# An encoder step on one core: latent keys prepared during the last projections, rotations on ACT, held columns of the output projection, and the third phase's tiles placed over x's

## The chip, the cores and the metric

The kernel runs on one core of one Trainium2 chip. What is measured is the device time of one execution in microseconds (us), given as the median of several runs. A profile of one further execution goes with it. The engines are named as in the profile: PE (TensorE matmuls), PEld (its weight loads), DVE (VectorE), ACT (ScalarE), POOL (GpSimd) and SP (SyncE, which issues all the DMAs of this kernel).

## The reference, cut to what matters

One layer of a streaming encoder runs on 592 rows: 16 meta tokens, 512 prompt frames and 64 sample frames, with 128 cached rows behind the sample. Model width is 2048. Everything is fp32.

```
h = rmsnorm(x);  z = h @ w_in                  # q, k, v of 8 "diff" heads; cq (512), ckv (256), kr (64)
cq = rmsnorm(cq); qm = cq @ w_uq               # 8 latent heads: 128 plain + 64 rotary columns each
ckv = rmsnorm(ckv); krope = rope(kr)           # both are outputs too
diff heads:   p = softmax(q1 k1 + bias) - lam softmax(q2 k2 + bias);  o = rmsnorm(p v)
latent heads: km, vm = ckv @ w_ukv;  p = softmax(qn km + rope(qr) krope);  o = p vm
x = x + concat(o_diff, o_latent) @ w_out
x = x + (silu(h2 @ w_gate) * (h2 @ w_up)) @ w_down,  h2 = rmsnorm(x);  y = rmsnorm(x)
```

## The kernel before, in words

Every fp32 operand of a matmul is held as a pair: `hi` (an fp32r copy made by ACT) and `lo` (the remainder, by one DVE subtraction). A product is three passes: hi*hi, hi*lo, lo*hi. `split` (L170) makes a pair, `mm3` (L195) issues the three passes for each half of the columns, so six matmuls for one 128x128 block of weights and 576 columns.

The work around the change has three stages.

First, the projections (`projections`, L704) go through the 8 diff heads (q, k, v columns of w_in), then through the latent columns in the order 4, 5, 6, 0, 1 (ckv, ckv, kr, cq, cq), and last through cq columns 2 and 3 together, in 16 blocks of rows; each finished block calls `release(kc)` (L814), which gives that block's room in the tile of x to something else. While they run, the attention of the diff heads is woven in.

Second, the latent stage. `query_norm` (L836) sums the squares of the four cq tiles (POOL adds, then a matmul with ones) and makes the row `rsq`. `latent_keys` (L862) splits the latents and the cache and rotates the shared key; `latent_rows` (L901) turns latents and key back into rows for the outputs, closes two pools, opens `aq` in their place and sets `named`. `heads` (L1077) then goes through the 8 latent heads: `rotary_queries` (L992) for each pair, `queries_keys` (L1023) for each head, `pair_values` (L1007) for each pair, and a spawned `latent_attend` (L1043) that makes scores in 5 blocks, then the product with the values (`probabilities_times_values`, L231). `mix_out` (L938) is the first half of the output projection (the diff heads' part): 16 columns of 8 `mm3` each, and it is the fill for all gaps.

PE's order is written out by a planner (`Streams`, L45): generators yield delays or lists of things they wait for, each has a rank, the ready one of the lowest rank goes next, and the matmuls that it issues move the planned clock. `mix_out` has rank 30, `heads` 20, the attention of a head its number. PSUM banks are planned too: `ps` (2 of them), `sp` (1), `tp` (1), `po` (1). The order of ACT, DVE, POOL and SP in these stages is chosen by the compiler; that of PE is kept as planned.

Third, from L1244, the second half of the output projection: the latent heads' results are loaded from `mspill`, split, and multiplied with the lower half of w_out (`fetch`, L1261), 16 columns, and the operands for the feed-forward part are made beside it. The rest (from L1309) is the feed-forward part, three quarters of the time.

`rope` (L847) makes the rotation of a tile: four DVE operations on 32 partitions each, that read one quarter and write another (times a sign and the sine), one POOL product with the cosine, one DVE addition.

Of the kernel before, what the change touches and what calls it, by code (L numbers as in the profile page):

```python
# [30 lines left out]
H = 8  # L31
# [10 lines left out]
WR_BUFS, WH_BUFS, Z_BUFS, OT_BUFS = 2, 2, 3, 4  # L42

# [87 lines left out]
def encoder_step(  # L131
# [99 lines left out]
    def probabilities_times_values(pt_b, p5, vkeys, vpast, pool, tbank, pso, pace, done):  # L231
# [19 lines left out]
        for g, blocks in enumerate((((0, 0), (0, 1), (0, 2), (0, 3)), ((1, 0), (1, 1), (1, 2), (1, 3)),  # L251
# [3 lines left out]
            yield from st.take("tp")  # L255
# [20 lines left out]
            st.give("tp", 1.9)  # L276
# [78 lines left out]
    with ExitStack() as ph:  # L355
# [271 lines left out]
        def diff_attend(h, khs, kl, vh, vl):  # L627
# [8 lines left out]
            for b in range(5):  # L636
# [30 lines left out]
                (vh[:, 5, :], vl[:, 5, :]), ap, tbank, pso, 1.0,  # L667
# [12 lines left out]
            if h < H - 1:  # L680
                store(mspill[h], o32)
            else:
                yield [released[h]]
                mixh[h], mixl[h] = (x_room(h, w, f"mx{w}{h}")[:, 0:TQ] for w in "hl")
                split(mixh[h], mixl[h], o32)
# [3 lines left out]
        def key_latent_norm():  # L689
# [6 lines left out]
            for i in range(2):  # L696
                V.scalar_tensor_tensor(zs[4 + i], zs[4 + i], gkv[:, i:i + 1], r, op0=ALU.mult, op1=ALU.mult)

# [5 lines left out]
        def projections():  # L704
            for h in range(H):
# [39 lines left out]
            for i in (4, 5, 6, 0, 1):  # L745
# [8 lines left out]
                if i == 6:  # L754
# [5 lines left out]
                    st.spawn(2, key_latent_norm())  # L760
# [23 lines left out]
            st.spawn(2, latent_keys(), [att[H - 1]])  # L784
# [6 lines left out]

        normed = []
# [6 lines left out]
        def query_latent(i, z):  # L799
            cqh[i], cql[i] = (zl.tile([P, TQ], F32R, name=f"cq{w}{i}", tag=f"q{i // 2}{i % 2}{t}")  # L800
                              for w, t in zip("hl", "sz"))
            split_scaled(cqh[i], cql[i], z, gq[:, i:i + 1])
# [3 lines left out]
            else:  # L806
                S.activation(z, z, AF.Square)
                G.tensor_tensor(sqs[0], sqs[0], z, op=ALU.add)
# [4 lines left out]

        def release(kc):  # L814

            released[kc]["done"] = True
            if kc < H - 1:
                assert att[kc]["done"]
                mixh[kc], mixl[kc] = (x_room(kc, w, f"mx{w}{kc}")[:, 0:TQ] for w in "hl")
                load(f32(mixl[kc]), mspill[kc])  # L820
                S.activation(mixh[kc], f32(mixl[kc]), AF.Copy)
                V.tensor_tensor(mixl[kc], f32(mixl[kc]), f32(mixh[kc]), op=ALU.subtract)
            elif kc == 10:
                for w, name, src in (("h", "cos", c_cos), ("l", "sin", c_sin)):
                    at_x[name] = x_room(kc, w, name, F32)
                    load(at_x[name], src)
            elif kc == 11:
                at_x["rsq"] = x_room(kc, "h", "rsq", F32)[:, 0:TQ]
                at_x["kr"] = x_room(kc, "l", "kr", F32)
            elif kc in (12, 13):  # L830
                i = kc - 12
                oth = slice(64 - i * 64, 128 - i * 64)
                rq.append([x_room(kc, w, f"rq{i}{w}")[:, 0:TQ] for w in "hl"])
                load(f32(rq[i][1][oth, :]), qmask[oth, :])

        def query_norm():  # L836
            yield 5.0
            yield from st.take("sp")
            pq = sbig("pq")
            for i in range(2):  # L840
                PE.matmul(pq[:, i, 0:QH], ones, sqs[0][:, i * QH:(i + 1) * QH], start=True, stop=True)
            v = ztile("v")[:, 0:TQ]
            V.tensor_scalar(hv(v, TQ), ev(pq, QH), 1.0 / QL, EPS, op0=ALU.mult, op1=ALU.add)
            st.give("sp", 1.5)
            rsqrt(at_x["rsq"], v)

        def rope(dst, z):  # L847
# [14 lines left out]
        def latent_keys():  # L862

            rkh = keys_room("kh0", "rkh")
# [20 lines left out]
            kr = at_x["kr"]  # L885
# [4 lines left out]
            st.give("tp", 3.0)  # L890
            rope(kr, zs[6])
# [3 lines left out]
            yield 9.0  # L895
            st.spawn(1, latent_rows())

        named = dict(done=False)
        aq, probs = [], []

        def latent_rows():  # L901

            kr = at_x["kr"]
            for j in range(5):
                o, n = tok[j]
                yield from st.take("tp")
                pn = tbank("pn")
                for i in range(2):
                    PE.transpose(pn[0:n, i * P:(i + 1) * P], zs[4 + i][:, o:o + n], ident)
                PE.transpose(pn[0:n, 256:320], kr[0:64, o:o + n], ident[0:64, 0:64])  # L910
                nn = ztile("nn")
                V.tensor_copy(nn[0:n, 0:320], pn[0:n, 0:320])
                r = min(n, NM + SEQ - o)
                store(nckv_p[o:o + r, :], nn[0:r, 0:KVL])
# [870 lines left out]
```

## Time and profile before

| | us |
|---|---|
| median of 3 runs (2456.5 to 2459.86) | 2457.34 |
| the profiled execution's own time | 2460.72 |
| its span, first to last instruction | 2458.9 |
| PE busy | 2384.6 (97%) |
| DVE busy | 1801.3 (73%) |
| ACT busy | 1162.6 (47%) |
| POOL busy | 717.9 (29%) |

The span's mean granted TensorE clock is 0.989. The latent stage begins at about 533 us of the span (end of the projections), the third stage's first matmul starts at 830.30, and the feed-forward part begins at about 938.

How to read the rows that follow. A row of the table by stretches gives a stretch's start and end, its width, the busy time of each engine with its count of instructions, the granted clock (PEclk, 1.00 is full speed), the busy share of the DMA engines and GB/s. A row of the timeline has start, duration, engine, line, operation, out<-in, shapes and count, and in brackets how long the engine had been idle before and what released it. Line L124 is a helper's line, so tiles are told apart by their names: `ps`, `sp`, `tp`, `po`, `pv`, `pq` are PSUM tiles, `mw` the weights of the latent heads, `mxh`/`mxl` the diff heads' pairs, `t` the rotated part, `kr` the rotated key, `zq`/`zr` the rotary queries, `m` the PSUM tile of the third stage.

### The profile page before, as it was taken

What the parts mean: (1) busy time and instruction counts of PE and PEld (TensorE: products, weight loads), DVE (VectorE), ACT (ScalarE), POOL (GpSimd) and SP (SyncE); (2) the same over time, 40 slices, a digit from 0 to 9 for tenths busy, and PEclk for the clock granted to TensorE, in tenths of its full rate; (3) what the DMA queues carried; (4) which work ended last, traced back from release to release, by engine and by line L of the source; (5) the groups of instructions that cost most, each with busy time, mean ns of one, the idle gap of its engine ahead of it and who ended that gap; (6) DMA issues with size and microseconds to landing.
All of it is one profiled execution on the core that took longest, in us unless ns stands there. A gap on an engine that the chain in (4) does not pass through costs nothing.

```text
span 2458.9 us, 44446 instructions
## 1 busy us (share of the span) xinstructions
PE 2384.6 (97%) x17539; PEld 2343.2 (95%) x17539; DVE 1801.3 (73%) x2828; ACT 1162.6 (47%) x2205; POOL 717.9 (29%) x550
## 2 busy tenths in 40 slices
PE   8999999988999799999999999999999999999998
PEld 7999999988999699999999999999999999999998
DVE  5665556675666478778888888788887888888874
ACT  5554544443444355445554555555555433333445
POOL 0000000010000154644545545445454322222223
PEclk9999999999999899999999999999999999999999
DMA  8533323243231454334334443443444875744332
GB/s 244 143 91 87 83 81 98 81 121 107 87 105 63 157 175 132 110 118 156 131 130 150 137 141 133 147 160 117 141 154 157 278 233 179 236 160 164 106 116 82
DMA packets 330990, 337.49 MB, mean 137 GB/s; under 512 B 22287, under 2 KB 273942, under 8 KB 330750
## 3 DMA queue, kind: packets, MB, share of 16 engines
q1 hardware_dynamic: 330782, 334.66, 42.5%
q8 instruction: 137, 2.24, 0.4%
q14 instruction: 71, 0.58, 0.1%
HBM read 264.98 MB, written 72.97 MB: 137 GB/s over the span
## 4 chain that ended last, share of the span: by engine, by line
PE 65%; DVE 4%; DMA 2%; POOL 1%; issue 1%; ACT 1%; DVEq 0%; POOLq 0%; ACTq 0%; SPq 0%
PE m L1234 35%; PE m L1238 18%; PE m L199 5%; PE ps L107 4%; DVE wl L124 1%; PE po L107 1%; PE sp L107 1%; DVE b L124 1%; DMA raw<-in_ffn_w_down 1%; PE tp L111 1%; POOL ws L1203 1%; DMA raw<-in_ffn_w_gate 1%; DMA raw<-in_ffn_w_up 1%; PE pv L107 1%; DMA x<-mspill 0%
## 5 line engine op out<-in xcount | busy, mean ns | idle before, releaser
L1234 PE MATMUL m<-b,wh 128*128 128x288 f32 x7168 | 1048.6, 295 | 6.4 <-DVE y L124 3.2
L1234 PEld LDWEIGHTS m<-b,wh 128*128 128x128 f32 x7168 | 984.7, 189 | 8.3 <-ACT wh L124 7.2
L1238 PE MATMUL m<-b,wl 128*128 128x288 f32 x3584 | 580.8, 297 | 3.0 <-DVE wl L124 2.7
L1203 POOL TENSOR_TENSOR ws<-raw 128x512 f32<-128x512 f32 (+1 forms) x258 | 374.8, 1463 | 541.7 <-DVE wl L124 275.3
L1238 PEld LDWEIGHTS m<-b,wl 128*128 128x128 f32 x3584 | 514.4, 189 | 4.6 <-DVE wl L124 4.3
L124 ACT ACTIVATE wh<-ws 128x512 fp32r<-128x512 f32 (+1 forms) x340 | 283.4, 845 | 386.6 <-PE m L1234 242.0
L124 DVE TENSOR_TENSOR wl<-ws,wh 128x512 fp32r<-128x512 f32 (+1 forms) x340 | 391.0, 1161 | 84.4 <-ACT wh L124 82.2
L124 ACT ACTIVATE wh<-raw 128x512 fp32r<-128x512 f32 x387 | 227.4, 620 | 287.6 <-PE m L1234 250.8
L124 DVE TENSOR_TENSOR wl<-raw,wh 128x512 fp32r<-128x512 f32 x387 | 357.3, 949 | 7.6 <-ACT wh L124 7.0
L107 PE MATMUL ps<-xh,wh 128*128 128x296 f32 (+1 forms) x960 | 218.0, 309 | 2.2 <-ACT wh L124 2.2
L107 PE MATMUL ps<-xl,wh 128*128 128x296 f32 (+1 forms) x960 | 209.3, 299 | 1.5 <-DVE xl L124 1.5
L124 DVE TENSOR_TENSOR y<-y,m 128x288 f32<-128x288 f32 x312 | 140.1, 451 | 91.4 <-PE m L1238 71.3
L107 PE MATMUL ps<-xh,wl 128*128 128x296 f32 (+1 forms) x928 | 201.7, 299 | 0.1
L124 DVE TENSOR_TENSOR ws<-ws,raw 128x512 f32<-128x512 f32 (+1 forms) x129 | 110.6, 860 | 76.5 <-POOL ws L1203 74.2
L107 PEld LDWEIGHTS ps<-xh,wh 128*128 128x128 f32 x960 | 156.0, 191 | 6.2 <-ACT wh L124 2.9
L107 PEld LDWEIGHTS ps<-xl,wh 128*128 128x128 f32 x960 | 156.4, 190 | 2.2 <-DVE xl L124 2.2
L107 PEld LDWEIGHTS ps<-xh,wl 128*128 128x128 f32 x928 | 150.7, 189 | 0.8 <-DVE wl L124 0.8
L124 DVE TENSOR_TENSOR wl<-wr,wh 128x1024 fp32r<-128x1024 f32 (+1 forms) x108 | 114.7, 1062 | 37.6 <-ACT wh L124 34.1
L124 ACT ACTIVATE wh<-wr 128x1024 fp32r<-128x1024 f32 (+1 forms) x110 | 101.6, 924 | 69.7 <-PE ps L107 37.6
L1422 POOL TENSOR_TENSOR c<-c,rb 128x576 f32<-128x576 f32 x44 | 70.5, 1604 | 169.0 <-ACT c L124 169.0
L630 POOL MEMSET bias<- 64x64 f32 x8 | 1.2, 144 | 384.0 <-DMA bias<-tsk 277.4
L124 ACT ACTIVATE parts<-c 128x1 fp32r<-128x1 f32 x252 | 81.2, 322 | 41.9 <-DVE c L124 36.2
(349 smaller groups left out, 3108.3 us busy)
## 6 DMA issues: line engine op xcount, KB each, us to landing
raw<-in_ffn_w_gate SPq DMA_DIRECT2D x44, 1024.0 KB, 6.1
raw<-in_ffn_w_up SPq DMA_DIRECT2D x44, 1024.0 KB, 6.3
raw<-in_ffn_w_down SPq DMA_DIRECT2D x39, 1024.0 KB, 5.5
partspill<-parts SPq DMA_DIRECT2D x126, 288.0 KB, 2.1
b<-partspill SPq DMA_DIRECT2D x126, 288.0 KB, 6.1
wr<-in_w_in SPq DMA_DIRECT2D x60, 512.0 KB, 4.1
wr<-in_w_out SPq DMA_DIRECT2D x16, 512.0 KB, 4.3
wr<-in_w_out SPq DMA_DIRECT2D x32, 256.0 KB, 3.1
```

Source lines behind the costliest of these rows:

```text
L107: self.tc.keep_in_program_order(self.pe.matmul(out, lhsT, rhs, start=start, stop=stop))
L111: self.tc.keep_in_program_order(self.pe.transpose(out, in_, identity))
L124: ins = issue(*args, **kwargs)
L199: PE.matmul(outs[i], w, x[i], start=start and p == 0, stop=stop and p == 2)
L630: G.memset(bias[0:64, 464:528], -BIG)
L1203: engine.tensor_tensor(w[:, k:k + m, :], pick(xs), pick(ys), op=op)
L1234: PE.matmul(banks[p], wh[:, k, :], x, start=first and new and k == 0 and x is hi, stop=False, skip_group_check=not new)
L1238: PE.matmul(banks[p], wl[:, k, :], hi, start=False, stop=last and k == n - 1, skip_group_check=not new)
L1422: G.tensor_tensor(g[:, f, :], g[:, f, :], rb2, op=ALU.mult)
```

## The change: what it does, and its diff

1. The latents' norm (`key_latent_norm`) is spawned after column 5 instead of 6, and makes the ckv rows (transposes, copies and stores) itself. `latent_keys` is spawned when the last diff head's scores are planned, and needs the norm. The shared key is rotated as soon as `release(7)` gave it room, its two remainders are made on POOL instead of DVE, and its rows go out in one bank. `latent_rows` becomes `latent_room`, which only swaps the pools.
2. `rope`: four copies on ACT (scale = sign) move the quarters, one DVE product with the sine on all 128 partitions, POOL's product first, one DVE addition.
3. Query norm: the squares are issued before the split, from tiles of their own; the sum uses the `tp` bank in two halves.
4. `heads`: the rotary parts are written for each head (`rotary_parts`), an even head's projections wait for the scores of head h-2 rather than of h-1, and the values of a pair come after both heads' projections. The first rotary projection uses the `sp` bank.
5. The last head: its scores alternate between `sp` and `ps` banks, its transposes between `tp` and `sp`.
6. `mix_out` holds its last two columns (HELD = 2) until all of the heads' projections and values are planned (`prepared`).
7. Rooms over x's are dealt out anew (which tile lies over which block of x), the diff heads' results are loaded at releases 8 to 14 instead of 0 to 6.
8. Third stage: its pools move from one side of the memory to the other, all tiles are laid out beforehand, the latent heads' results are loaded straight into the tile of `lo`, and the first two blocks of w_out go through rooms of their own. Later pools (`fr`, `fw`, `fs`, `fb`, `yy`) change sides too.

```diff
-            yield from st.take("tp")
+            bank, tbank = tbanks[g % len(tbanks)]
+            yield from st.take(bank)
...
+                if h == H - 1:
+                    st.spawn(2, latent_keys(), [scored[H - 1], att[H - 2]])
...
+                    if i == 5:
+                        key_norm.append(st.spawn(2, key_latent_norm()))
...
-            st.spawn(2, latent_keys(), [att[H - 1]])
+            st.spawn(1, latent_room(), [att[H - 1]])
...
-            split_scaled(cqh[i], cql[i], z, gq[:, i:i + 1])
...
-                S.activation(z, z, AF.Square)
-                G.tensor_tensor(sqs[0], sqs[0], z, op=ALU.add)
+                sq = ztile("sq")[:, 0:TQ] if i == 3 else ap.tile([P, TQ], F32, name="sq")
+                S.activation(sq, z, AF.Square)
+                G.tensor_tensor(sqs[0], sqs[0], sq, op=ALU.add)
+            split_scaled(cqh[i], cql[i], z, gq[:, i:i + 1])
...
         def rope(dst, z):
+            G.tensor_tensor(dst, z, at_x["cos"][:, c], op=ALU.mult)
             for a in range(0, P, 32):
                 b = a ^ 32
-                V.scalar_tensor_tensor(t[b:b + 32, :], z[a:a + 32, :], sign[a:a + 32, :], at_x["sin"][a:a + 32, c],
-                                       op0=ALU.mult, op1=ALU.mult)
-            G.tensor_tensor(dst, z, at_x["cos"][:, c], op=ALU.mult)
+                S.activation(t[b:b + 32, :], z[a:a + 32, :], AF.Copy, scale=sign[a:a + 32, :])
+            V.tensor_tensor(t, t, at_x["sin"][:, c], op=ALU.mult)
             V.tensor_tensor(dst, dst, t, op=ALU.add)
...
-                sub_lo(rkl[i][both[i], 0:T], kr[both[i], :], rkh[both[i], 0:T])
+                G.tensor_tensor(rkl[i][both[i], 0:T], kr[both[i], :], f32(rkh[both[i], 0:T]), op=ALU.subtract)
...
         def mix_out():
...
             for i in range(KC):
+                if i == KC - HELD:
+                    yield [prepared]
...
-                yield from st.take("sp")
-                n, W, view, vw = scores(b, sbig(), [
+                bank = "ps" if h == H - 1 and b % 2 else "sp"
+                yield from st.take(bank)
+                n, W, view, vw = scores(b, sbig() if bank == "sp" else pjt(), [
...
+            tbanks = [("tp", tbank)] + [("sp", lambda: sbig("tp2")[:, 0, :])] * (h == H - 1)
...
         def heads():
             yield 3.0
-            for h in range(H):
-                j = h // 2
-                if h % 2 == 0:
-                    yield from rotary_queries(j)
-                if h == 0:
-                    yield [named]
-                if h >= 2:
-                    yield [asked[h - 2]]
-                qk = yield from queries_keys(h)
-                lat[h] = st.spawn(h, latent_attend(h, *qk), [asked[h - 1]] if h else [])
-                yield 0.5
-                if h % 2 == 0:
+            for j in range(H // 2):
+                zr = yield from rotary_queries(j)
+                for i in range(2):
+                    h = 2 * j + i
                     if j:
-                        yield [lat[h - 1]]
-                    yield from pair_values(j)
+                        yield [asked[h - 2]]
+                    rotary_parts(i, zr)
+                    if h == 0:
+                        yield [named]
+                    qk = yield from queries_keys(h)
+                    lat[h] = st.spawn(h, latent_attend(h, *qk), [asked[h - 1]] if h else [])
+                    yield 0.5
+                if j:
+                    yield [lat[2 * j - 1]]
+                yield from pair_values(j)
+            prepared["done"] = True
...
-    ma, close_ma = pool("ma", "right")
+    ma, close_ma = pool("ma")
...
-    mixh, mixl = [], []
+    mixed = [[mx.tile([P, TQ], F32R, name=f"m{w}{h}") for w in "hl"] for h in reversed(range(H))][::-1]
...
     for h in range(H):
-        m = ma.tile([P, TQ], F32, name="x", tag="x", bufs=3)
-        load(m, mspill[8 + h])
-        mixh.append(mx.tile([P, TQ], F32R, name=f"mh{h}"))
-        mixl.append(mx.tile([P, TQ], F32R, name=f"ml{h}"))
-        split(mixh[h], mixl[h], m)
+        load(f32(mixl[h]), mspill[8 + h])
+        S.activation(mixh[h], f32(mixl[h]), AF.Copy)
+        V.tensor_tensor(mixl[h], f32(mixl[h]), f32(mixh[h]), op=ALU.subtract)
...
+            if n < 2:
+                wr, wh, wl = (bc.tile([P, 2, QH], t, name=f"b{p}_5").rearrange("p a b -> p (a b)")[
+                    :, 0:4 * P].rearrange("p (k c) -> p k c", k=4) for p, t in zip(((1, 2, 4), (5, 6, 3))[n], (F32, F32R, F32R)))
...
-    fr, close_fr = pool("fr")
-    fw, close_fw = pool("fw")
+    fr, close_fr = pool("fr", "right")
+    fw, close_fw = pool("fw", "right")
```

More of the change, by code (lines that the diff above doesn't have):

```diff
@@ L812, in encoder_step, with mix_rooms @@
         at_x = {}
+        def mix_rooms(h):
+            mixh[h] = (x_room(h, "h", f"mxh{h}") if h < 7 else x_room(7, "l", f"mxh{h}"))[:, 0:TQ]
+            mixl[h] = x_room(8 + h, "l", f"mxl{h}")[:, 0:TQ]
         def release(kc):
             released[kc]["done"] = True
[L817 to L831, printed above, removed]
+            if kc == 0:
+                at_x["rsq"] = x_room(0, "l", "rsq", F32)[:, 0:TQ]
+            elif kc in (5, 6):
+                name, src = (("cos", c_cos), ("sin", c_sin))[kc - 5]
+                at_x[name] = x_room(kc, "l", name, F32)
+                load(at_x[name], src)
+            elif kc == 7:
+                at_x["kr"] = x_room(kc, "h", "kr", F32)
+            if kc in (9, 11):
+                i = (kc - 9) // 2
@@ L993, in rotary_queries @@
             wh, wl = weights4(w_uq4[:, :, 2 * j:2 * j + 2, 128:192], [P, 4, 2, 64])
[L994 removed]
+            z = yield from q_project(wh, wl, "zq", "ps" if j else "sp")
             yield 1.5
```

170 lines of the change are left out of this document (103 added, 67 removed).

## The prediction

> **What bounds the kernel now.** I read the page's busy times first, which make PE the busiest engine by far, then cut the span into stretches, to see where PE loses time. Lost PE time is the width less busy time times granted clock, since a matmul at half clock is busy twice as long.
>
> ```profile
> core 0: us, PE busy (x) PEld busy (x) DVE busy (x) ACT busy (x) POOL busy (x), PEclk, DMA share, GB/s
> ...
> 497.00:533.00 36.00, 34.94 (x254) 33.31 (x252) 21.66 (x37) 18.45 (x32) 3.78 (x2) 1.00 0.54 161
> 533.00:580.00 47.00, 34.71 (x198) 30.66 (x197) 35.51 (x49) 15.02 (x24) 7.21 (x13) 0.85 0.33 94
> 580.00:806.00 226.00, 221.43 (x1618) 212.25 (x1616) 135.92 (x264) 92.67 (x207) 5.11 (x3) 1.00 0.28 85
> 806.00:821.00 15.00, 11.00 (x44) 7.47 (x42) 4.76 (x11) 3.89 (x11) 0.00 (x0) 0.66 0.05 20
> 821.00:835.00 14.00, 4.70 (x21) 4.73 (x22) 5.83 (x8) 5.34 (x8) 0.00 (x0) 0.51 0.75 230
> 835.00:937.00 102.00, 101.13 (x746) 99.47 (x746) 78.23 (x114) 58.00 (x113) 46.73 (x44) 1.00 0.58 178
> 937.00:950.00 13.00, 10.45 (x65) 9.86 (x64) 11.75 (x17) 7.70 (x15) 6.33 (x6) 0.87 0.59 188
> ```
>
> Lost are 1.1 us in 497:533, 17.5 in 533:580 (47 - 34.71 x 0.85), 4.6 in 580:806, 7.7 in 806:821 (15 - 11.00 x 0.66), 11.6 in 821:835 (14 - 4.70 x 0.51), 0.9 in 835:937 and 3.9 in 937:950 (13 - 10.45 x 0.87): 47 us in all. PE's work itself doesn't change, so 47 us is the most that the change can win. Three places hold 37 of them: the start of the latent stage, the last head's end, and the step into the third stage.
>
> In the first, the waits of PE and the load on DVE say why:
>
> ```profile
> PE pn L111 <- DVE nn L124: 4.3, 3, 3.0
> PE pq L107 <- POOL sqs L808: 2.7, 1, 2.7
> PE ps L107 <- DVE xo L124: 2.1, 1, 2.1
> PE pv L107 <- DVE mw L124: 1.5, 1, 1.5
> ```
>
> ```profile
> 535.00:560.00 25.00, 17.53 (x112) 16.01 (x111) 24.56 (x32) 7.08 (x13) 6.00 (x3) 0.93 0.30 88
> ```
>
> DVE is busy 24.56 of 25 us there, and three of the four longest waits end at a DVE tile. So DVE is the bound for 25 us, while PE has 16 columns of fill to draw on that it can't use: their banks and the heads behind them wait for DVE.
>
> **Part by part: the start of the latent stage.** What DVE does in 533:580, by group:
>
> ```profile
> L124 DVE SCALAR_TENSOR_TENSOR t<-zl,sign,sin 32x592 f32<-32x592 f32 x4 | 4.3, 1083 | 0.1
> L124 DVE SCALAR_TENSOR_TENSOR t<-zq,sign,sin 32x576 f32<-32x576 f32 x4 | 4.3, 1073 | 0.1
> L124 DVE TENSOR_TENSOR wl<-wr,wh 128x1024 fp32r<-128x1024 f32 x3 | 3.7, 1221 | 0.0
> L124 DVE COPY nn<-pn 128x320 f32<-128x320 f32 x4 | 2.0, 488 | 1.9 <-PE pn L111 1.9
> ```
>
> ```profile
> L124 ACT ACTIVATE rq0h<-zr 64x576 fp32r<-64x576 f32 x4 | 2.7, 686 | 15.4 <-DVE zr L124 15.4
> ```
>
> The key's rotation (4.3 us) and the row copies (2.0) move ahead of 533, where DVE has 14 us free (36 - 21.66). The first query rotation drops from 4.3 us of DVE to one product; its four copies go to ACT at about 0.69 each (the ACT row, 64 partitions; the trace has none of 32 partitions that change place, and the other near row is DVE's own 1.08; I take ACT's, since the engine is the same), 2.7 us (4.3 at the other bound) on an engine that is busy 15 of 47. So about 10 us leave DVE's 35.5, and DVE stops being the bound. The chain that is left is the query norm:
>
> ```profile
> 537.40 3.74 POOL L808 TENSOR_TENSOR sqs<-sqs,z 128x576 f32<-128x576 f32 x2 [7.87 <-ACT z L124]
> ...
> 539.92 1.85 DVE L124 SCALAR_TENSOR_TENSOR t<-zl,sign,sin 32x592 f32<-32x592 f32 x1
> ...
> 541.20 2.29 PE L107 MATMUL pq<-sqs,ones 128*128 128x288 f32 x4 [2.69 <-POOL sqs L808]
> ...
> 551.47 0.75 DVE L124 SCALAR_TENSOR_TENSOR rsq<-v,rsq 128x576 f32<-128x576 f32 x1
> ...
> 567.42 0.85 PE L107 MATMUL ps<-cqh,mw 128*128 128x288 f32 x2
> ...
> 580.06 0.23 PE L107 MATMUL sp<-km,qnh 128*128 128x144 f32 x1
> ```
>
> Squaring before splitting lets each square skip an ACT copy and a DVE subtraction of about 0.75, so POOL's two adds (1.87 each) end near 538.3 instead of 541.1. From there: the sum 1.2 us (half of the 2.29 at half clock), four DVE steps of 0.75, two ACT steps of 0.69, some handovers: `rsq` near 545 instead of 552.2. The rotation: POOL beside ACT 2.7, two DVE steps 1.5, the parts 2: near 552 head 0's projections start, which were at 567.42 behind the rows' transposes (the 4.3 us of `pn` waits, now gone). Scores start about 16 us earlier than 580.06. In between PE needs fill, and has it:
>
> ```profile
> 591.74 0.43 PE L107 MATMUL ps<-mxh,wh 128*128 128x288 f32 x2
> 592.00 0.42 PE L107 MATMUL ps<-mxl,wh 128*128 128x288 f32 x2
> ```
>
> Two matmuls take 0.265 us, so a column (48) is 6.4 us and all 16 are 102. What stays: part of the `pq` wait (0 to 2.7, I take 1, and 1 more as its halves share one bank with a DVE read between), the weights' and the `xo` wait in part (1.5), and slow clock behind them (2): 5.5 of 17.5. Gain 12.0; bounds 3 (only the norm's 3 us) and 16.
>
> The clock: no PE wait of this stretch is over 3.0 us, yet it ran at 0.85 on average, a loss of 5 us. The Trainium skill, TensorE: Matmul & The Clock Gate, "What's actually happening", says that the clock halves after an idle window of about 3.4 us. By that rule the waits that I leave over would cost no clock, and the gain would be an estimated 14; by the trace shorter gaps do it, and I keep the 2.
>
> The two subtractions moved to POOL, with the cosine product, are some 5.6 us of POOL (three times 1.87) before 533, where POOL is busy 3.78 of 36. If they came late they would hold DVE too: the quarter at 539.92, beside POOL's adds, took 1.85 us, against a mean of 1083 ns for the four. The Trainium skill, SBUF — State Buffer, "Who interferes with whom", says that a DVE instruction with two SBUF inputs and a POOL instruction that reads SBUF share a port, and whichever starts later waits for the whole of the other; the trace agrees with that one row. By it the two subtractions would take up to an estimated 3.7 us from the gain if they met DVE's busy stretch. I take 0, because DVE has 14 us free where they run, and keep 3.7 for the range.
>
> **The projections' end.** Ten row transposes, five copies and six stores move in ahead of 533, the diff heads' loads move later. The nearest rows are the `pn` waits, at most 4.3 us if all came along; between two of them lies fill here. I take a loss of 0.8, bounds 0 and 4.3. Release 14 instead of 6 is 8 blocks of 12 matmuls later, 12.7 us. The last of these loads has one block (1.6 us) and six `mm3` of the first column (4.8) as cover; it needs a load and a split, 4.7 us by the rows of the third stage below. Without that cover it costs these 4.7.
>
> **The middle.** Two held columns take 12.8 us of fill out of 580:806. Against that an even head's projections no longer wait for the head before, so more of the heads' own work is ready at a time. I take a loss of 0.9, bounds 12.8 and a gain of 3.
>
> **The last head.** PE runs out of fill near 806 and then goes from wait to wait through the product with the values. With two held columns (12.8 us) against 7.7 lost, and banks that alternate, nearly all is covered: gain 7.0, bounds 3 and 7.7.
>
> **The step into the third stage.**
>
> ```profile
> 820.82 0.32 SPq L124 DMA_DIRECT2D mspill<-o  x1
> 823.04 1.27 SPq L124 DMA_DIRECT2D x<-mspill  x3
> ...
> 830.30 0.82 PE L199 MATMUL m<-mh,wh 128*128 128x288 f32 x2 [9.77 <-DMA x<-mspill]
> ```
>
> ```profile
> x<-mspill SPq DMA_DIRECT2D x8, 288.0 KB, 3.3
> ```
>
> Before, all the loads of the third stage stand in SP's queue behind the last head's store: 2.2 us to land, then 7.3 us until the first matmul, and the clock of 821:835 is 0.51. After, seven of the eight results and the first two weight blocks lie in rooms that are free earlier, and can be loaded and split under the last head. Only the eighth still goes out and back: store 2.2, load 3.3, split 1.4 (0.69 on ACT, 0.75 on DVE), so 6.9 us, against 42 matmuls on the other seven (5.6 us) and whatever is left of the fill. I leave 2.5 of 11.6: gain 9.1, bounds 1.5 and 11.6.
>
> **The feed-forward part.** Pools change sides; its 3.9 us at 937:950 may move by up to 2.6 either way, I take 0. No other step changes.
>
> Sum: 12.0 - 0.8 - 0.9 + 7.0 + 9.1 = 26.4 us. The profiled execution took 2460.7 (span 2458.9 and 1.8 around it), so 2434.3 for one like it; the median of the runs is 3.4 lower, so 2431.
>
> **Rivals.** (A) The fill runs out before the held columns are let go, and PE stands for those 12.8 us in the middle. For: the earlier start takes more fill before 580, and 580:806 has only 4.6 us of slack as it is. Against: with projections ready earlier the heads need less of it. 2431 + 12.8 = 2444.
>
> (B) The third stage's loads still wait for the last store, because the spill is seen as one thing or SP's queue has them in that order. For: all three loads left together 2.2 us after the store. Against: their rooms change, and one queue entry that waits would look the same. It leaves 1.5 of 9.1: 2439.
>
> (C) Slower: the values of a pair come after the odd head's projections, and the even head's product waits for them.
>
> ```profile
> 780.87 0.28 PE L107 MATMUL pv<-mw,cl 128*128 128x256 f32 x1
> ...
> 790.42 0.49 PE L107 MATMUL ps<-ch,mw 128*128 128x360 f32 x2
> ```
>
> Here the values ended at 781.1 and the odd head's projections at 790.9, ten us later less a gap: about 8.8 us for each of four pairs is 35 us, if PE has nothing else: 2466. It decides from 6.6 us a pair (26.4 / 4). For: the product follows its values closely. Against: those projections now run under the scores of the head before.
>
> (D) DVE was busy but not binding: the query norm alone holds the heads, and 533:580 gives 3 of 12: 2440.
>
> **How the numbers follow.** The forecast 0.56, A 0.14, B 0.12, D 0.06, A, B and D together 0.04 (2461, no change), C 0.08. A measurement of this kernel can tell about 0.2% (5 us) from no change: faster 0.88, same 0.04, slower 0.08. The range goes from 2416 (the upper bounds of start and step together) to 2448 (past A, and past B with D); it leaves out C, the sum of A, B and D, and a little below.
>
> **What would show it.** PE's lost time in the stage from the end of the projections to the first scores under 8 us, the first scores some 30 us after that end instead of 47; no `t<-zq` on DVE; PE at clock 1.00 through the last head; the `mspill` loads issued before the last store, and under 3 us of wait before the third stage. Wrong would be a stretch of over 5 us without fill before the held columns, products that wait for `vl` tiles, or loads still in one row behind the last store.

## The result, and the profile after

The changed kernel takes 2440.1 us (median of 4 runs, 2436.8 to 2440.5) against 2456.9 of the kernel before on the same chip (4 runs, 2454.7 to 2459.9): a ratio of the means of 0.9928, 95% interval 0.9911 to 0.9945. The profiled execution took 2440.5 us with a span of 2437.7. Single executions of some variants below came out 8 to 16 us under the median of the same kernel with the granted clock within 0.003 of the others', so medians are compared, and of the version with everything, whose profiled execution is such a one (2413.3 us, and 9870 matmuls in the 1300 us from 1000 on against 9766 in the changed kernel), only the time up to the feed-forward stage is read.

This is the view of busy times by stretch of the changed kernel (columns as in the prediction; the last three are PE's granted clock, the DMA share and GB/s):

```profile
497.00:535.00 38.00, 37.63 (x276) 35.82 (x274) 22.57 (x42) 20.73 (x36) 6.30 (x4) 1.00 0.52 145
535.00:574.00 39.00, 30.99 (x210) 30.24 (x210) 26.73 (x35) 18.59 (x28) 6.37 (x13) 0.91 0.41 127
574.00:790.00 216.00, 213.55 (x1555) 204.59 (x1556) 128.05 (x260) 101.84 (x221) 5.19 (x3) 1.00 0.28 86
790.00:803.00 13.00, 11.40 (x75) 9.49 (x74) 3.45 (x6) 3.39 (x8) 0.00 (x0) 0.98 0.37 121
803.00:820.00 17.00, 3.40 (x16) 3.43 (x17) 8.06 (x12) 7.91 (x12) 0.00 (x0) 0.51 0.86 275
820.00:922.00 102.00, 101.49 (x755) 100.29 (x753) 77.12 (x112) 55.90 (x110) 47.35 (x44) 1.00 0.51 154
922.00:935.00 13.00, 10.35 (x55) 9.86 (x56) 11.16 (x16) 7.30 (x15) 5.68 (x5) 0.76 0.66 208
```

Lost PE time, reckoned as in the prediction (width less busy time times clock), before and after:

| stretch | before | after |
|---|---|---|
| projections' end | 1.1 | 0.4 |
| start of the latent stage | 17.5 | 10.8 |
| middle | 4.6 | 2.5 |
| last head | 7.7 | 1.8 |
| step into the third stage | 11.6 | 15.3 |
| third stage | 0.9 | 0.5 |
| first 13 us of the feed-forward stage | 3.9 | 5.1 |

The first six rows give back 12.1 us. On the trace's own time axis the feed-forward stage's first matmul comes at 922.3 instead of 938.3, 16.0 earlier. Of the 3.9 between the two numbers, 1.3 may lie in the first 497 us (PE idle for 22.96 before, 21.69 after; the clock is left out, as it is given to 0.01 only, which is 5 us there), and 2.6 I cannot place.

These gains are measured against one profile of the kernel before. A second one (at the end of the experiments) has the feed-forward stage begin at 936.7, so a single trace is good to 1.6 us at that point, and it loses less in two of the rows.

Two holes hold most of what is left. The waits of PE between 500 and 960 us (us in total, times, longest):

```profile
PE m L200 <- ACT b L125: 14.0, 1, 14.0
PE ps L108 <- DVE z L125: 7.3, 2, 7.0
PE pq L108 <- POOL sqs L827: 1.0, 1, 1.0
```

The many waits at the start of the latent stage (rows, `xo`, `mw`) are gone and one is new: the output projection's first matmul waits 7.0 us for a PSUM bank, where it waited 0.76 before. Both banks hold a query column, and DVE frees them late, by the evacuation `z<-ps` (the operation that takes a finished result out of its bank). PE before, then PE and DVE of the changed kernel, in order of time (start, duration):

```profile
533.96 0.50 PE L107 MATMUL ps<-mxh,wh 128*128 128x288 f32 x2 [0.76 <-DVE z L124]
```

```profile
541.99 0.82 PE L108 MATMUL ps<-mxh,wh 128*128 128x288 f32 x2 [6.97 <-DVE z L125]
...
565.31 0.42 PE L108 MATMUL ps<-cqh,mw 128*128 128x288 f32 x2
...
573.88 0.34 PE L108 MATMUL sp<-km,qnh 128*128 128x144 f32 x1
```

```profile
539.75 0.76 DVE L125 TENSOR_TENSOR mxl<-mxl,mxh 128x576 fp32r<-128x576 f32 x1 [0.27 <-ACT mxh L125]
...
541.10 1.42 DVE L125 TENSOR_TENSOR z<-ps,rb 128x576 f32<-128x576 f32 x2
```

In DVE's order the evacuation stands behind the splits of the diff heads' results, which wait for loads, because the change moved these from releases 0 to 6 to releases 8 to 14. The first scores still come earlier, at 573.9 instead of 580.1.

The second hole is the step into the third stage. SP's queue of the changed kernel (start, duration of the issue):

```profile
798.33 0.32 SPq L125 DMA_DIRECT2D x1spill<-xo  x1
802.91 0.32 SPq L125 DMA_DIRECT2D mspill<-o  x1
805.03 3.86 SPq L125 DMA_DIRECT2D ml<-mspill  x8
809.00 1.86 SPq L125 DMA_DIRECT2D b<-in_w_out  x2
```

All eight results are still loaded 2.1 us after the last store, as in the prediction's rival B, and now all eight go ahead of the first weight block (three did before), so the third stage's first matmul comes at 816.6, 14.0 us after PE's last one, against 9.8 before.

### The profile page after: what moved, and what is told of

Read it like the earlier page. It is cut to its first block, busy times and chain, and to the rows that moved or that the text cites. A ratio compares the mean times of both kernels' runs of the same rounds, so it can differ in the third digit from the quotient of the medians.

```text
span 2437.7 us, 44467 instructions
## 1 busy us (share of the span) xinstructions
PE 2372.2 (97%) x17539; PEld 2337.2 (96%) x17539; DVE 1779.7 (73%) x2814; ACT 1175.8 (48%) x2225; POOL 714.7 (29%) x552
## 4 chain that ended last, share of the span: by engine, by line
PE 88%; DVE 4%; DMA 3%; ACT 2%; issue 1%; POOL 1%; SPq 0%; DVEq 0%; POOLq 0%; ACTq 0%
PE m L1270 37%; PE ps L108 20%; PE m L1274 18%; PE m L200 5%; PE po L108 2%; PE sp L108 2%; DVE wl L125 1%; PE tp L112 1%; DMA raw<-in_ffn_w_down 1%; DVE b L125 1%; PE pv L108 1%; SPq L125 0%; PE m L1666 0%; DMA wr<-in_w_in 0%; POOL ws L1239 0%
## 5 line engine op out<-in xcount | busy, mean ns | idle before, releaser
L1274 PE MATMUL m<-b,wl 128*128 128x288 f32 x3584 | 570.3, 295 | 2.4 <-DVE wl L125 2.4
L1579 POOL TENSOR_TENSOR c<-c 128x576 f32<-128x576 f32 x42 | 73.7, 1755 | 85.6 <-DVE c L125 81.6
```

Of the source, the lines that this page charges most:

```text
L1274: PE.matmul(banks[p], wl[:, k, :], hi, start=False, stop=last and k == n - 1, skip_group_check=not new)
L1579: G.tensor_tensor(w[:, f, :], w[:, f, :], g[:, f, :], op=ALU.mult)
```

## The experiments

The kernel before, measured again with each group of variants, has medians of 2456.8 to 2458.0, so each variant's median is set against the one measured with it, and that difference against the changed kernel's 16.8. The ratios are of means. "To the feed-forward stage" is the start of that stage's first matmul in the one profile, less the changed kernel's 922.3; it leaves out some 1500 us that the variants leave alone (the third stage as before changes only the pools' sides there), but it rests on single traces.

| variant | median | ratio to before, 95% | against the change | to the feed-forward stage |
|---|---|---|---|---|
| columns first | 2437.7 | 0.9916 [0.9895, 0.9937] | -2.3 | -0.4 |
| weights first | 2437.3 | 0.9924 [0.9912, 0.9936] | -2.7 | -2.1 |
| last result elsewhere | 2437.2 | 0.9924 [0.9911, 0.9936] | -2.8 | -3.7 |
| both rooms, weights first | 2430.4 | 0.9897 [0.9882, 0.9911] | -9.6 | -9.3 |
| the same, columns first, norm later | 2426.1 | 0.9863 [0.9843, 0.9882] | -14.2 | -9.3 |
| third stage as before | 2438.8 | 0.9925 [0.9913, 0.9937] | -1.6 | -1.9 |
| last head plain | 2440.9 | 0.9926 [0.9908, 0.9943] | +0.6 | +1.2 |
| latent keys late | 2446.9 | 0.9945 [0.9923, 0.9967] | +6.6 | +9.6 |
| rotation on DVE | 2443.6 | 0.9934 [0.9919, 0.9948] | +2.4 | +7.3 |
| values after the even head | 2452.0 | 0.9976 [0.9966, 0.9985] | +10.8 | +11.9 |
| that and last head plain | 2446.0 | 0.9952 [0.9939, 0.9964] | +4.8 | +9.2 |

Half an interval is 2 to 5 us, so single differences of 2 or 3 us are read from the traces or not at all. The last two columns differ by up to 4.9 us (rotation on DVE), and the last one is good to about 1.6, so differences below that are not told from nothing. The rooms dealt out anew, the rest of the query norm's change and the even heads' earlier start were not undone alone.

**Columns first.** The two query columns leave their banks before the sixteenth release, and the splits of heads 4 to 6 come last:

```
                    if kc == KC - 1:
                        columns = [query_columns(p) for p in ps]
                    release(kc)
...
            for h in range(4, H - 1):
                split_mix(h)
```

> The changed kernel with one order altered: the two query columns are evacuated right after the last projection's matmuls, ahead of the rows of the sixteenth release, and the splits of the diff results of heads 4 to 6 come after them. Theory (the 6.97 us hole before the first output-projection matmul is DVE's order: the evacuations of z, which free the PSUM bank, stand behind seven splits whose loads land late): the hole shrinks to 1 to 2 us, and since PE is busy for over 98% of the 216 us that follow, the whole kernel gains 5 to 6 us, to about 2434.5. Rival (the hole is the late landing of the results' loads, which the first output-projection matmul needs anyway): the wait only changes its name, gain 0 to 1. Second rival (the heads' chain sets the end of the stage, not PE's work): the hole goes and comes back as idle time before the last head, gain 0 to 1.

Its waits of PE in the same stretch:

```profile
PE pq L108 <- POOL sqs L832: 4.9, 1, 4.9
PE ps L108 <- DVE z L125: 2.9, 2, 2.6
```

DVE's order did make most of the hole: it fell from 7.0 to 2.6. But of the 4.4 us another wait took 3.9, and the feed-forward stage began 0.4 us earlier. The first rival holds in a form that I had not put: what takes over is not the loads but the query norm's matmul, which stands next in PE's order and waits for POOL's sum of squares.

**The third stage's three edits.** Weights first moves `for n in range(2): fetch(n)` ahead of the loads of the results. Last result elsewhere changes one room:

```
-            o32 = x_room(7, "h", "o32", F32)[:, 0:TQ]
+            o32 = (ztile("o32") if h == H - 1 else x_room(7, "h", "o32", F32))[:, 0:TQ]
```

Both rooms has both edits, and the first two weight blocks in the tiles of all the later ones (the branch `if n < 2` never taken).

> The changed kernel with one order altered: the first two blocks of the output projection's weights are loaded ahead of the eight latent results, from the same rooms. Theory (the 14.0 us before the third stage's first matmul is the queue: eight results of 295 KB each go ahead of the first weight block, all behind the last head's store): the first matmul comes at about 810 instead of 816.6, and is then paced by the results at about 1 us each, so the step costs 4 to 6 us less, to about 2435. Rival (the bytes bound it: all eight results have to land before the first column is done, in whatever order): gain 0 to 1.5.

> The changed kernel with one room altered: the last head's result is evacuated into a tile of the pool az instead of x's pool; spill, loads and weights stay. Theory (x's pool is released as a whole, so every load into its former rooms waits for the last reader of any room in it, and that reader is the last head's own store): six or seven of the eight result loads leave before that store, the weights' two blocks still wait for the last head's end, the first matmul comes about 5 to 7 us earlier, time about 2434. Rival (my prediction's rival B, first reason: the spill is seen as one thing, so that every load of it waits for the last store into it): the loads still leave after the store, no change (within 1 us). Rival (B, second reason: the queue's order): no change either.

> The changed kernel with the last head's result in az, the first two weight blocks in the rooms that all later blocks use (over x's pool, free before the last head's end), and these blocks loaded ahead of the results. Theory (whole-pool release and the queue's order together make the 15.3 us): weights and results 0 to 6 land under the last head, the first matmul follows the last head's by 2 to 4 us, and 10 to 13 us go, to about 2428. Rival (other traffic bounds it: the 1 MB of the gate's weights is loaded in the same 8 us, so that the loads merely crowd each other and the last head's store): gain not above that of the two single edits, 5 to 7 us.

SP's queue and the first matmul with weights first:

```profile
804.87 0.32 SPq L125 DMA_DIRECT2D mspill<-o  x1
807.11 0.94 SPq L125 DMA_DIRECT2D b<-in_w_out  x2
808.09 4.16 SPq L125 DMA_DIRECT2D ml<-mspill  x8
```

```profile
813.34 0.82 PE L200 MATMUL m<-mh,b 128*128 128x288 f32 x2 [8.76 <-ACT mh L125]
```

With the last result in another room:

```profile
798.18 0.32 SPq L125 DMA_DIRECT2D ml<-mspill  x1
...
799.29 2.00 SPq L125 DMA_DIRECT2D ml<-mspill  x4
804.66 0.32 SPq L125 DMA_DIRECT2D mspill<-o  x1
805.02 2.20 SPq L125 DMA_DIRECT2D ml<-mspill  x3
807.33 0.93 SPq L125 DMA_DIRECT2D b<-in_w_out  x2
```

With both:

```profile
797.54 0.94 SPq L125 DMA_DIRECT2D wr<-in_w_out  x2
...
799.06 1.51 SPq L125 DMA_DIRECT2D ml<-mspill  x3
803.07 0.32 SPq L125 DMA_DIRECT2D mspill<-o  x1
803.43 3.33 SPq L125 DMA_DIRECT2D ml<-mspill  x5
```

```profile
804.31 0.82 PE L200 MATMUL m<-mh,wh 128*128 128x288 f32 x2 [1.52 <-ACT mh L125]
```

In the second variant neither the spill nor the program order differs from the changed kernel, only the room of the last head's result, and five loads leave before that head's store. So the loads did not wait for the data, nor for the spill as one thing, and in the changed kernel as it was built none of the eight loads lands over that result's room either (only the `hi` copy of the eighth lies there): they waited for x's pool as a whole, whose last reader was the store of a result that lay in it. Each edit alone shortens the wait (14.0 to 8.8 and 9.4) and moves little, since the other reason then holds the first matmul: with weights first it is the first result that is late, with the results early it is the weights. With both, and the weights' own rooms changed as well, 1.5 us are left, and the gain to the feed-forward stage, 9.3, is more than 2.1 and 3.7 together. What the third of these edits brings alone was not run. The last rival, that the loads merely crowd each other, is out, as the gain is above its 5 to 7. It is a little under the theory's 10 to 13: PE runs at half clock for its first 4.7 us there, which costs 2.3.

**Everything together.** Both rooms and the columns first, with the query norm later in PE's order:

```
         def query_norm():
-            yield 4.0
+            yield 9.0
```

> The version with both rooms changed and the weights first (2430.4 us), plus the query columns' evacuation ahead of the sixteenth release, plus the query norm's two matmuls put later in PE's order (a pause of 9 instead of 4 ahead of them). Theory (in the version with the columns first, the 7.0 us hole became 2.6 and a 4.9 us wait of the query norm's matmul for POOL's sum took most of the gain, because PE runs in order; with output-projection matmuls ahead of it that wait is covered): both waits together fall to about 3 us, time 2424 to 2426. Rival (the start's chain over POOL and the query norm decides when the latent heads begin, and PE has no more work to put under it): the lost time appears as another wait before the first scores, gain under 1.5, 2429 or more.

The median, 2426.1, meets the theory; the profile does not. The waits did go, the first matmul of the output projection comes after 2.8 us, and none is for POOL. But the first scores come at 578.7 instead of 573.8, the fill ends 2.9 us earlier (the last `x1spill` store at 795.7 against 798.6), the third stage's first matmul comes at 804.9 against 804.3, and the feed-forward stage starts at the same 912.9. What is saved at the start is then missing as fill at the end. Whether the columns' order gains up to 4 us or nothing stays open: the profiled execution is the odd one named above, and the two versions' intervals touch. As the fastest version measured it is 31 us, or 1.3% by the medians, below the kernel before (the ratio of the means, 0.9863, has the odd execution in it).

**The third stage as before**, from its pools to the end of the kernel:

```
-    ma, close_ma = pool("ma")
+    ma, close_ma = pool("ma", "right")
...
-        load(f32(mixl[h]), mspill[8 + h])
+        m = ma.tile([P, TQ], F32, name="x", tag="x", bufs=3)
+        load(m, mspill[8 + h])
```

> The changed kernel with the third stage's rooms, loads and pool sides as in the kernel before: one part undone, all others kept. Theory (this part lost time: its stretch cost 15.3 us lost against 11.6 before, since eight result loads instead of three now go ahead of the first weights): 3 to 4 us faster than the changed kernel if nothing else hangs on it, about 2436.5, with the first third-stage matmul 13 to 14 us after the last head's last one reduced to 9 to 11. Rival (the prediction's step: this part gains 9.1): slower, 2449. Rival (the part loses at the step and gains in the feed-forward stage by its pool sides, where the profile of the changed kernel is 5.2 us shorter): about 2441, no change.

The first matmul waits 9.2 us instead of 14.0, and the feed-forward stage starts 1.9 us earlier and is as long (1515.2 against 1515.5). The prediction's step, a gain of 9.1, is refuted; by the trace the part as written costs about 2 us, little more than two traces of one kernel differ by. In the medians 1.6 us are within the uncertainty.

**Last head plain**: `HELD = 0`, `bank = "sp"`, and one bank for the transposes.

> The changed kernel with the last latent head as before: no held columns, its scores and transposes through one bank each. Theory (the prediction's step: 7.0 us; the two traces' lost time there 7.7 and 1.8): 5 to 7 us slower than the changed kernel, 2445 to 2447, with the last head's waits back in the profile. Rival (held columns only move PE's work, so that what is gained under the last head is lost where they were held): 0 to 2 us slower.

The rival is nearer: 1.2 us to the feed-forward stage, 0.6 by the medians, neither clear of noise. The fill does run out earlier, but the tail is far shorter than before all the same. The next pair says why.

**The values' order**: `pair_values(j)` after the even head's projections, once with the rest of the change and once with the last head plain as well.

```
                    yield 0.5
-                if j:
-                    yield [lat[2 * j - 1]]
-                yield from pair_values(j)
+                    if i == 0:
+                        if j:
+                            yield [lat[2 * j - 1]]
+                        yield from pair_values(j)
```

> The changed kernel with the heads' order of before in one point: a pair's values are made right after the even head's projections, not after the odd head's. Theory (the stretch of the middle gained 2.1 us and the last head is covered because the values now come late, so that the fill lasts longer): 1 to 3 us slower than the changed kernel, with waits back in the middle. Rival (the prediction's rival C, the late values hold up the even head's product): faster by 2 or more. Second rival (PE's fill covers either order): within 1 us.

> The changed kernel with both undone: a pair's values after the even head, no held columns, one bank each for the last head's scores and transposes. Theory (undoing the last head's part alone cost only 0.8 us, 1.2 up to the feed-forward stage, because the order of the values had already moved the fill to the end): together they lose the 5.9 us that the two traces show at the last head, the clock falls to half there as before, 5 to 7 us slower than the changed kernel, 2445 to 2447. Rival (the fill lasts longer for another reason, the earlier start of the heads above all): no more than the two single edits together, 1 to 3 us slower.

Here the theory was far too low, and rival C was wrong in sign: the late values are worth 10.8 us with held columns and 4.2 without (4.8 less 0.6), or 11.9 and 8.0 by the traces. The last key projection, in the changed kernel and in the variant with both undone (in the kernel before it is the row at 790.42, in the prediction):

```profile
756.34 0.49 PE L108 MATMUL ps<-ch,kw 128*128 128x360 f32 x2
```

```profile
784.39 0.49 PE L108 MATMUL ps<-ch,kw 128*128 128x360 f32 x2
```

With the values late, the odd head's projections no longer stand behind them, its scores can start 28 us earlier (the last of them begin at 770.5 against 800.5), and less of the last head is left when the fill ends. From the last `x1spill` store to the last head's own store it takes 13.7 us in the kernel before (807.15 to 820.82; 11.8 in its second profile), 4.6 in the changed kernel, and in last head plain and in both undone:

```profile
795.28 0.32 SPq L125 DMA_DIRECT2D x1spill<-xo  x1
803.31 0.32 SPq L125 DMA_DIRECT2D mspill<-o  x1
```

```profile
798.18 0.53 SPq L125 DMA_DIRECT2D x1spill<-xo  x1
...
812.88 0.32 SPq L125 DMA_DIRECT2D mspill<-o  x1
```

8.0 and 14.7: the order does most of it, the held columns and banks the rest. Lost PE time says the same: 7.8 us at the last head with both undone (795 to 813), 3.5 in last head plain (788 to 803.6), 1.8 in the changed kernel. And held columns without the new order are the slowest of these. This is PE in the variant with only the values' order undone:

```profile
764.93 0.42 PE L108 MATMUL ps<-mxh,wl 128*128 128x288 f32 x2
769.23 0.46 PE L108 MATMUL pv<-mw,ch 128*80 128x256 f32 x2 [2.70 <-DVE vl L125]
...
782.42 0.43 PE L108 MATMUL ps<-mxh,wh 128*128 128x288 f32 x2
```

For 17.5 us there is no fill, because two columns are held: rival A, in the one version that has its condition. They then end with the last head, not before it, and the wait ahead of the third stage grows to 18.0.

**Latent keys late**: `yield key_norm + [att[H - 1]]` at the head of `latent_keys`, so that their work falls into the start of the stage again.

> The changed kernel with the latent keys made only after the last diff head, as before, all else kept: their transposes, rotation, splits and rows fall into the start of the latent stage again. Theory (the start was bound by DVE and PE waiting for it, and the keys' work was a part of that queue): the start loses most of what it gained, 5 to 8 us slower than the changed kernel, 2445 to 2448. Rival (after the change the start is bound by the query columns alone, and the keys' work fits beside the output projection's matmuls): 0 to 2 us slower. Rival (the late keys also let the query columns go ahead of them on DVE, so that the 7.0 us hole closes): faster by up to 3.

Its waits of PE:

```profile
PE ps L108 <- DVE xo L125: 7.8, 1, 7.8
PE ps L108 <- DVE z L125: 5.8, 2, 5.4
PE pq L108 <- POOL sqs L827: 2.8, 1, 2.8
```

The theory holds: 6.6 us by the medians, 9.6 by the trace. The hole before the first column stays (the third case, that it closes, is out), and a wait of 7.8 us for DVE comes behind it.

**Rotation on DVE**: the four products with sine in place of the copies on ACT.

> The changed kernel with the rotation as before: four products with sine of 32 rows each on DVE in place of four copies on ACT and one product. Theory (after the change PE's hole at the latent stage's start ends with the query columns' evacuation, ahead of any rotation, and behind it the output projection's matmuls cover the heads' chain): the first scores come 1 to 3 us later, PE loses no more, 0 to 1.5 us slower. Rival (the prediction's reason: DVE was the bound of the start, and 3.5 us of it a rotation are what the move bought): 3 to 5 us slower, with longer waits of PE for DVE before the first scores.

The trace points to a loss above my theory's (7.3 us; the 2.4 of the medians are within their uncertainty), and in another place than the rival's. The first scores come 1.8 us later (575.7), but 3.6 us are lost in 580:785, where each pair rotates once more (lost 5.6 against 2.0), with waits such as this, which the changed kernel does not have there:

```profile
PE tp L112 <- DVE pk1l L125: 2.7, 3, 1.4
```

**The kernel before once more**, for its feed-forward stage: a second profile, of a single run.

> The kernel before once more, for a second profile of it. The first shows 1520.6 us from the feed-forward stage's first matmul to the end, and the changed kernel and its variants 1512.4 to 1515.5, with no part of the change in that stage that would explain it. If this is the pace of one execution, a second one lies at 1513 to 1517; if the change did it, at 1520 again. Time 2452 to 2461.

2454.0 us, span 2452.2, feed-forward stage from 936.7: 1515.5 us, as long as the changed kernel's. The 1300 us from 1000 on, first profile and second:

```profile
1000.00:2300.00 1300.00, 1294.71 (x9709) 1292.55 (x9708) 1064.71 (x1454) 621.79 (x1122) 570.46 (x397) 1.00 0.48 159
```

```profile
1000.00:2300.00 1300.00, 1297.98 (x9751) 1296.64 (x9751) 1069.63 (x1465) 626.24 (x1129) 561.81 (x398) 1.00 0.48 160
```

It is the pace of one execution, not the change: 9709 and 9751 matmuls of the same kernel in the same time.

The second profile also says how far the stretches before that stage can be trusted. The start of the latent stage and the last head in it:

```profile
533.00:580.00 47.00, 35.78 (x213) 32.40 (x212) 36.40 (x49) 15.96 (x26) 7.20 (x13) 0.89 0.34 98
806.00:819.00 13.00, 8.85 (x43) 6.18 (x42) 4.76 (x11) 3.77 (x11) 0.00 (x0) 0.87 0.06 23
```

Lost are 15.2 and 5.3 us (13 - 8.85 x 0.87), against 17.5 and 7.7 in the first profile.

## Why the prediction was right, and where it was not

The sign was right, and the time lies in the range, 9 us above the forecast: of the 26.4 us forecast, 16.0 came up to the feed-forward stage. Two steps failed, the cover at the projections' end and, far dearer, the step into the third stage, which came out with the wrong sign; gains in the middle that were not forecast made up a little of it. That the time fell beside rival B's 2439 is luck: B's price was too small and other terms were off too. The lower end of the range is also misstated: the upper bounds of start and step together give 4.0 + 2.5, so 2424.5, and 2416 needs all the upper bounds at once; the measured time lies inside either way. Step by step, measured by the table of lost time:

- **The start, 12.0 forecast, 6.7 measured** (4.4 against the second profile of before). The first reason holds: the keys' work moved ahead is worth 6.6 us by the medians. The second, rotating on ACT, is worth 2.4 by the medians, which noise could make, and 7.3 by the trace, of which 3.6 lie in the middle. The ACT copy with changed partitions, which the trace of before did not show and for which I took 0.69, took 0.77:

```profile
L125 ACT ACTIVATE t<-zq,sign 32x576 f32<-32x576 f32 x4 | 3.1, 774 | 0.1
```

  The forecast of `rsq` near 545 and of head 0's projections near 552 was 10 to 13 us early (555.1 and 565.3): the chain began at 541, when the columns left their banks, not at 535, when PE was done with them. So the first scores came 6 us earlier than before, not 16.
- **The projections' end, a loss of 0.8 forecast.** This is the first step that failed. "The last of these loads has one block (1.6 us) and six mm3 of the first column (4.8) as cover" takes it that the first column runs beside the loads. It cannot: its bank is held by a query column whose evacuation stands behind those very splits on DVE. The cost was 7.0 us, above the 4.7 that I gave for a missing cover; it falls into the start's row of the table and is most of what the start lacks. The columns-first run shows that 4.4 of it are DVE's order. That run also shows that the query norm (rival D) is next in line, so that the hole alone is worth little.
- **The middle, a loss of 0.9 forecast, a gain of 2.1 measured.** The held columns cost nothing there, as the values' order sets the odd head's work free; without that order they do (rival A).
- **The last head, 7.0 forecast, 5.9 measured** (3.5 against the second profile of before). The size was near, the reason right only in part: I gave it to held columns and banks, and undoing them loses 1.7 us there (3.5 against 1.8) and 1.2 up to the feed-forward stage; the values' order, which I weighed only as a danger, does most of the rest. That the size came near is luck.
- **The step into the third stage, 9.1 forecast, a loss of 3.7 measured.** This is the second step that failed, and with 12.8 us between forecast and measurement the dearest. The prediction's own sign of it, loads still in one row behind the last store, is in the trace. Rival B came true, by neither of its reasons as I put them. Not the spill but the pool of the last head's result held the loads, and the queue's order came on top of it: eight results ahead of the weights. "Lie in rooms that are free earlier" was read off the tiles' places; what counts is the last reader of the whole pool. Rival B's price was wrong too. It left 1.5 of gain where the longer queue made a loss.
- **The feed-forward stage, 0 forecast.** 1515.5 us in the second profile of before and in the one of after. The 5.2 us between the two profiles first compared were the pace of one execution.
- **Rival C** is refuted: late values gain.
- **The clock.** I kept 2 us for a slow clock behind the remaining waits, by the trace and not by the rule of the Trainium skill. In the changed kernel it cost 2.8 of the start's 10.8 us (8.0 are idle), but behind a longer wait than any that I had left over. Here it falls:

```profile
538.00:539.00 1.00, 0.00 (x0) 0.00 (x0) 1.00 (x3) 1.00 (x2) 0.00 (x0) 1.00 0.12 26
539.00:540.00 1.00, 0.00 (x0) 0.00 (x0) 0.73 (x2) 1.00 (x3) 0.00 (x0) 0.81 0.00 0
540.00:541.00 1.00, 0.00 (x0) 0.00 (x0) 1.00 (x2) 0.29 (x1) 0.00 (x0) 0.50 0.00 0
```

PE stood from 535.0, the clock fell within the fifth microsecond, and it was full again before 547, within 5 us of the first matmul at 542.0. The Trainium skill, TensorE: Matmul & The Clock Gate, "What's actually happening", has the clock halve after an idle window of about 3.4 us and return after a busy one, and this hole agrees. The last head of the kernel before does not: its longest wait there is 1.73 us, and the clock is at 0.5 from 811 to the stage's end. In the second profile of that kernel, with a longest wait of 1.74 us there, it is at 0.5 from 810 to 813 only and full from 814 to the last matmul at 818. So the same waits cost different clock in two executions, and what makes it fall there is not settled.

## What to carry to other kernels

In this kernel a load into a room that was reused waited for the last reader of the whole pool that had held it, so one late store out of that pool undid the early release of all its other rooms; look for that reader before counting on the overlap. Early rooms help only if what the first matmul needs also stands first in the queue, and undoing one of two such reasons shows little of what undoing both brings. Before moving work ahead on an engine, list what it is moved in front of: a split that waits for a load, put ahead of an evacuation, holds a PSUM bank and with it PE.

## What was not expected of the hardware

A subtraction on DVE took 1.97 us where the same one, 2.6 us later, took 0.74, while POOL added two tiles. These are POOL and DVE in the columns-first variant:

```profile
543.67 1.40 POOL L832 TENSOR_TENSOR sqs<-sqs,sq 128x576 f32<-128x576 f32 x1
```

```profile
543.71 1.97 DVE L125 TENSOR_TENSOR mxl<-mxl,mxh 128x576 fp32r<-128x576 f32 x1
```

They start together, and DVE ends 0.6 us after POOL, about its own length. The Trainium skill, SBUF — State Buffer, "Who interferes with whom", has DVE and POOL share a port pair of which one holds the lock at a time, and these rows agree: POOL's work is not free for DVE, even off the critical path.
